# Hybrid attention, SSD and delta-net layer on one core: other PSUM banks for the first half's transposes, other buffers and a later request time around the second half's output projection

## The chip, the core and the metric

The kernel runs on one core of a Trainium2 chip. The metric is the device time of one execution in microseconds (us). TensorE (PE) does the matrix products, VectorE (DVE) and ScalarE (ACT) the elementwise work, GpSimd (POOL) some small operations; SyncE (SP) starts most transfers, and ACT starts the stores. Each engine takes its instructions in one fixed order, and each works through its own list without looking at what another engine's list holds, except where it waits for a semaphore.

## The reference

One layer on x of shape (1, 1024, 1024) in float32:

```
h    = rmsnorm(x);  p = h @ w_in
a    = sliding-window attention (4 heads, sinks, ALiBi)      256 columns
s    = Mamba-2 SSD                                           512 columns
g    = gated DeltaNet                                        256 columns
x1   = x + rmsnorm(concat[a, s, g] @ w_out)
h    = rmsnorm(x1)
out  = x1 + rmsnorm((silu(h @ w_gate) * (h @ w_up)) @ w_down)    FF = 2816
```

## The kernel before, in words

The 1024 rows are worked in two halves of 512 rows, each of 4 tiles of 128 rows (t = 0 to 3). Every matrix product is three passes over a float32r high part and low part ("hi" and "lo"): hi by hi, hi by lo, lo by hi. The split costs an ACT copy (hi) and a DVE subtraction (lo) for every operand block.

Phase 1 (`half`) makes the three mixers of a half and stores their outputs to DRAM as `mixd`. In the second half's order of work (`ORD[1]`) the steps end with `a0 a1 O a2 a3`: attention of tiles 0 and 1, then `O`, which is `block_first`, then attention of tiles 2 and 3. One attention tile (`att_tile`, twice a tile, once per key head) is: scores `as` on PE, mask and maximum on DVE (`asc`, `am`), exponentials on ACT, transposes `tp_p` on PE, a copy `apT` on ACT, the product `ao` on PE, the scaling `aout` on DVE, and a store of `aout` to `mixd`.

`block_first` is the first half's output projection: it multiplies the mixer output by `w_out` in four column groups g of 256 columns (`mm_o`, 24 matmuls for one g and one tile), and in g = 3, tile by tile, forms the first residual row `res`, its norm, a normalised row `o`, and after t = 1 and t = 3 the transposes `tp_f` of two tiles, whose evictions give `hhi_m` (ACT) and `hlo_m` (DVE). The early FFN products of the first half follow: `e00p` to `e11p` (`ffn_early`, pairs 0 and 1, 96 matmuls of 512 columns).

PSUM has eight banks. In phase 1 they are four pools of two: "mm" (projections, `mm_o`), "gd", "sd" (DeltaNet and SSD; "sd" also `ao`) and "at" (`as`, `tp_p`). A pool hands its two buffers out in the order in which the program is written, so an `as` of tile 2, written after `block_first`, gets a buffer that a `tp_f` written before it has held.

Phase 2 begins with the second half's output projection: the mixer output is read back (`mixn`, L1026 to L1030), transposed (`tp_m`, by `split_T`) into `mhi` and `mlo`, and multiplied by `w_out` (again `mm_o`, g = 0 to 3). Between the groups stand the early FFN products of pairs 2 to 5 (`e20p` to `e51p`, 192 matmuls). Then the rows are transposed (`tp_f`, L1096), combined into the operands of a Strassen form (`hx`, `T1` to `T4`), and 11 FFN pairs follow (`fg0p`, `fu0p` and on), whose raw weights `fg0r`, `fu0r` (512 KB loads) go into the four "nat" buffers of `npool`. In the kernel before, `mixn` lies in "nat" too, the second residual in "tmp", and all `w_out` pieces and all early weights pass through the three "wr" buffers of `wpool`.

What sets the order: the Tile framework's scheduler lists the instructions of every engine from the program, with priorities (`tc.high_priority`), buffer counts and a timeline model; the lists are fixed when the kernel is built.

## Time and profile before

| | us |
|---|---|
| median of 3 runs | 1301.12 (1297.75 to 1302.74) |
| the profiled execution | 1301.61 |
| its span, first to last instruction | 1299.8 |
| PE busy in the span | 1234.9 (95%) |
| DVE busy | 948.9 (73%) |
| ACT busy | 578.1 (44%) |
| mean granted PE clock | 0.970 of full speed |

The page cuts the span in 40 slices; PE is busy for 9 tenths or more in nearly all, and shows 6, 9 and 7 tenths in the three slices from 520 to 617 us, the crossing from the first half to the second, and 8 in the one from 682 to 715 us, the end of the second half's projection. Shares of busy time are averages over stages with different limits, so the stages are read apart from each other.

### The profile page before, as it was taken

The page shows a single profiled execution, that of the slowest core. Times are in us where ns is not written, and L with a number is a line of the kernel's source. Part 1 is how long each engine was busy: PE and PEld are TensorE (multiplying, and loading weights), DVE is VectorE, ACT ScalarE, POOL GpSimd, SP SyncE. Part 2 cuts the span into 40 slices and gives each one's busy share as a digit, 9 for nine tenths or more (in the row PEclk, how much of TensorE's full clock was granted, in tenths as well). Part 3 has the DMA queues.
Part 4 walks back from the last instruction along what each step waited for, and adds up shares of the span by engine and source line. Part 5 has one row for each costly group of instructions (what it writes and reads, how often), then busy time and mean ns, then how long its engine had stood idle before and what let it go on. Part 6 is the DMA issues. An engine that isn't in the chain of part 4 may idle for free.

```text
span 1299.8 us, 19149 instructions
## 1 busy us (share of the span) xinstructions
PE 1234.9 (95%) x6624; PEld 1028.3 (79%) x6624; DVE 948.9 (73%) x1898; ACT 578.1 (44%) x1269; POOL 225.3 (17%) x313
## 2 busy tenths in 40 slices
PE   5999999999998999697998999999999999999997
PEld 4878788887777889676996888888888887888885
DVE  5687996687799475644456999887777757767885
ACT  6454444445544343533436543433333343454561
POOL 3243554224355432200000000000000000000001
PEclk9899989999999999777998999999999999999999
DMA  7223332133323222535534356543333268676315
GB/s 234 74 70 85 86 89 65 48 103 89 96 77 80 76 91 74 174 96 196 170 106 139 121 189 224 187 138 114 100 111 99 72 217 311 190 218 230 98 57 194
DMA packets 161412, 168.57 MB, mean 130 GB/s; under 512 B 29566, under 2 KB 116890, under 8 KB 161316
## 3 DMA queue, kind: packets, MB, share of 16 engines
q1 hardware_dynamic: 143892, 133.53, 34.4%
q10 hardware_dynamic: 17424, 33.82, 7.0%
q8 instruction: 52, 0.85, 0.3%
q14 instruction: 44, 0.36, 0.1%
HBM read 127.21 MB, written 40.11 MB: 129 GB/s over the span
## 4 chain that ended last, share of the span: by engine, by line
PE 84%; DVE 7%; DMA 4%; ACT 2%; issue 1%; POOL 1%; ACTq 0%; SPq 0%; POOLq 0%; DVEq 0%
PE mm_p L1177 5%; PE mm_p L1179 5%; PE mm_p L1178 5%; PE mm_o L206 2%; PE mm_o L207 2%; PE mm_o L208 2%; PE gram L487 1%; DMA x<-in_x_dram 1%; PE mm_z L206 1%; DVE Tpr L513 1%; PE y L676 1%; DMA yb<-in_ffn_w_down_dram 1%; PE ao L755 1%; PE mm_z L207 1%; PE mm_z L208 1%
## 5 line engine op out<-in xcount | busy, mean ns | idle before, releaser
L169 POOL TENSOR_TENSOR rsq<-ssv,mhalf 128x1 f32<-128x1 f32 x32 | 19.8, 623 | 774.6 <-DVE ssv L259 774.5
L513 DVE TENSOR_TENSOR Tpr<-Tst,Wst 128x32 f32<-128x32 f32 (+30 forms) x62 | 49.0, 790 | 4.8 <-POOL Wst L508 4.1
L206 PE MATMUL mm_z<-wh_z,hhi_a 128*128 128x256 f32 x128 | 38.0, 297 | 0.0
L206 PE MATMUL mm_o<-wh_wo,hhi_m 128*128 128x256 f32 x128 | 36.5, 286 | 1.2 <-ACT junko L866 1.1
L207 PE MATMUL mm_o<-wl_wo,mhi 128*128 128x256 f32 x128 | 37.2, 292 | 0.2 <-DVE wl_wo L186 0.2
L208 PE MATMUL mm_o<-wh_wo,mlo 128*128 128x256 f32 x128 | 36.9, 290 | 0.0
L206 PE MATMUL mm_o<-wh_wo,mhi 128*128 128x256 f32 x128 | 36.8, 291 | 0.0
L208 PE MATMUL mm_z<-wh_z,hlo_a 128*128 128x256 f32 x128 | 36.6, 286 | 0.0
L207 PE MATMUL mm_z<-wl_z,hhi_a 128*128 128x256 f32 x128 | 36.6, 286 | 0.0
L208 PE MATMUL mm_o<-wh_wo,hlo_m 128*128 128x256 f32 x128 | 36.0, 281 | 0.0
L207 PE MATMUL mm_o<-wl_wo,hhi_m 128*128 128x256 f32 x128 | 35.9, 281 | 0.0
L185 ACT ACTIVATE wh_wo<-wr_wo 128x512 fp32r<-128x512 f32 x32 | 19.8, 629 | 34.0 <-DMA wr_wo<-in_w_out_dram 9.6
L186 DVE TENSOR_TENSOR wl_wo<-wr_wo,wh_wo 128x512 fp32r<-128x512 f32 x24 | 17.6, 743 | 16.8 <-ACT wh_wo L185 16.7
L515 DVE TENSOR_REDUCE Tst<-Tpr 128x16 f32<-128x32 f32 (+30 forms) x62 | 26.9, 433 | 0.6
L676 PE MATMUL y<-xs,sE 128*128 128x64 f32 x128 | 19.5, 283 | 7.6 <-DVE sE L669 7.6
L207 PEld LDWEIGHTS mm_o<-wl_wo,mhi 128*128 128x128 f32 x128 | 25.4, 198 | 0.8 <-DVE wl_wo L186 0.5
L206 PEld LDWEIGHTS mm_o<-wh_wo,mhi 128*128 128x128 f32 x128 | 25.2, 198 | 0.7 <-DVE mlo L236 0.3
L213 PE MATMUL mm_x<-hlo_a,wh_x 128*128 128x512 f32 x64 | 25.7, 402 | 0.0
L212 PE MATMUL mm_x<-hhi_a,wh_x 128*128 128x512 f32 x64 | 25.5, 399 | 0.0
L676 PEld LDWEIGHTS y<-xs,sE 128*128 128x128 f32 x128 | 18.2, 202 | 9.2 <-DVE sE L669 8.0
L206 PEld LDWEIGHTS mm_o<-wh_wo,hhi_m 128*128 128x128 f32 x128 | 24.1, 188 | 1.8 <-ACT junko L866 1.3
L214 PE MATMUL mm_x<-hhi_a,wl_x 128*128 128x512 f32 x64 | 25.5, 398 | 0.0
(1619 smaller groups left out, 4456.6 us busy)
## 6 DMA issues: line engine op xcount, KB each, us to landing
wr_wo<-in_w_out_dram SPq DMA_DIRECT2D x32, 256.0 KB
x<-in_x_dram SPq DMA_DIRECT2D x8, 512.0 KB
wr_x<-in_w_in_dram SPq DMA_DIRECT2D x16, 256.0 KB
wr_z<-in_w_in_dram SPq DMA_DIRECT2D x16, 256.0 KB
mixn<-mixd SPq DMA_DIRECT2D x16, 256.0 KB
resf<-x1d SPq DMA_DIRECT2D x8, 512.0 KB
wr_e<-in_ffn_w_gate_dram SPq DMA_DIRECT2D x12, 256.0 KB
wr_e<-in_ffn_w_up_dram SPq DMA_DIRECT2D x12, 256.0 KB
```

The costliest lines, as they stand in the source:

```text
L206: pe.matmul(ps, hi[:, tsl], whi, start=k == 0, stop=False)
L207: pe.matmul(ps, hi[:, tsl], wlo, start=False, stop=False)
L208: pe.matmul(ps, lo[:, tsl], whi, start=False, stop=k == len(wp) - 1)
L212: pe.matmul(ps, whi, hi, start=k == 0, stop=False)
L213: pe.matmul(ps, whi, lo, start=False, stop=False)
L214: pe.matmul(ps, wlo, hi, start=False, stop=k == len(wp) - 1)
L513: vec.tensor_tensor(pr[:, :, 0:i + 1], T[:, :, 0:i + 1], W[:, None, 0:i + 1, i].to_broadcast([P, CW, i + 1]), op=ALU.mult)
L515: vec.tensor_reduce(T[:, :, i], pr[:, :, 0:i + 1], axis=AX, op=ALU.add)
L676: pe.matmul(yd[:, j], E[:, j, :], xs[:, j], start=True, stop=True)
L1177: pe.matmul(ps[j], ah[:, s], bh, start=i == 0, stop=False)
L1178: pe.matmul(ps[j], ah[:, s], bl, start=False, stop=False)
L1179: pe.matmul(ps[j], al[:, s], bh, start=False, stop=i == NP - 1)
```

## The change

Five edits, all around the crossing from the first half to the second:

1. `block_first`'s transposes `tp_f` take buffers of "gd" and "mm" in place of "sd" and "at".
2. The second half's mixer output lies in eight "tmp" half-tiles. It is read by three transfers a tile in place of two (columns 512 to 1023, 256 to 511, and for all tiles last 0 to 255, the attention's columns), and transposed by one `split_T` over all four tiles (8 blocks of 128 x 512, the attention's blocks 0 and 1 last) in place of two over two tiles each (16 evictions of 128 x 256).
3. The second residual lies in "nat", one 512 KB load a tile in place of two of 256 KB.
4. The `w_out` pieces of g = 1 and g = 3 are split into "big" buffers in place of the six "wh" and "wl".
5. The raw early weights of pairs 2 to 5 go through "tmp" in place of "wr" and lose their high priority, and those of pairs 4 and 5 are written in the program after the projection, not in its g = 1.

```diff
--- before.py
+++ after.py
@@ -1,5 +1,5 @@
 import math
-from contextlib import ExitStack
+from contextlib import ExitStack, nullcontext
 
 import numpy as np
 import concourse.bass as bass
@@ -218,11 +218,11 @@
                  hp.tile([P, HT], F32R, tag="hlo", name=f"hlo_{name}{k}", bufs=KB))
                 for k in range(KB)]
 
-    def split_T(name, nats, t0, out, wcols, streams=("mm",)):
+    def split_T(name, nats, t0, out, wcols, streams=("mm",), ks=range(KB)):
 
         n = len(nats)
         s = slice(t0 * P, (t0 + n) * P)
-        for i, k0 in enumerate(range(0, KB, NT // n)):
+        for i, k0 in enumerate(ks[::NT // n]):
             p = mx(f"tp_{name}{t0}{k0}", streams[i % len(streams)])
             for e in range(NT // n):
                 for j in range(n):
@@ -879,7 +879,7 @@
                     else:
                         vec.tensor_scalar(o[t][e], src, r, None, op0=ALU.mult)
                 if t % 2:
-                    split_T(f"f{h}", [halves_of(o[t - 1]), halves_of(o[t])], t - 1, mT, 8, ("sd", "at"))
+                    split_T(f"f{h}", [halves_of(o[t - 1]), halves_of(o[t])], t - 1, mT, 8, ("gd", "mm"))
         return mT
 
 
@@ -905,12 +905,12 @@
             pe.matmul(ps, wlo[:, s], hi, start=False, stop=k == n - 1)
         return ps
 
-    def early_weights(w, i, e, tiles):
+    def early_weights(w, i, e, raw, tiles):
         n = f"e{i}{e}"
         parts = []
-        with tc.high_priority():
+        with tc.high_priority() if tiles is None else nullcontext():
             for h in range(2):
-                q = wpool.tile([P, WC], F32, tag="wr", name=f"wr_{n}{h}")[:, 0:HT]
+                q = raw(f"wr_{n}{h}")
                 q = q.rearrange("p (k c) -> p k c", k=4)
                 dma(q, w[h * HT:(h + 1) * HT, i * 256:i * 256 + P].rearrange("(k p) c -> p k c", p=P))
                 parts.append(split(f"{n}w{h}", q, tiles and tiles(f"{n}{h}")))
@@ -931,7 +931,7 @@
     mT_h0 = o0[0]
     for i in range(EARLY[0]):
         for e, w in enumerate((wg, wu)):
-            ffn_early(w, i, e, early_weights(w, i, e, None), lambda nm: mpool.tile(
+            ffn_early(w, i, e, early_weights(w, i, e, lambda nm: wpool.tile([P, WC], F32, tag="wr", name=nm)[:, 0:HT], None), lambda nm: mpool.tile(
                 [P, 4, P], F32, tag="Wn", name=nm, bufs=GT).rearrange("p a b -> p (a b)"), ("gd", "sd"))
     ph1.close()
 
@@ -950,6 +950,9 @@
 
     def big(nm, dt=F32R):
         return ph2.tile([P, HT], dt, tag="big", name=nm, bufs=BIG)
+
+    def big_pair(nm):
+        return big(f"{nm}h"), big(f"{nm}l")
 
     def tmp(nm):
         return ph2t.tile([P, HT], F32, tag="tmp", name=nm, bufs=TMP)
@@ -1022,18 +1025,26 @@
         return t
 
 
-    nats = []
+    nats, heads = [], []
     for t in range(NT):
-        mt = nat(f"mixn1{t}")
-        for e in range(2):
-            dma(mt[:, e * HT:(e + 1) * HT], mixd[NT + t][:, e * HT:(e + 1) * HT])
-        nats.append(cols_of(mt))
+        mt = [tmp(f"mixn1{t}{e}") for e in range(2)]
+        dma(mt[1], mixd[NT + t][:, HT:D])
+        dma(mt[0][:, 256:HT], mixd[NT + t][:, 256:HT])
+        nats.append(halves_of(mt))
+        heads.append(mt[0])
+    for t in range(NT):
+        dma(heads[t][:, 0:256], mixd[NT + t][:, 0:256])
     mT = [(big(f"mhi{k}"), big(f"mlo{k}")) for k in range(KB)]
-    for t0 in (0, 2):
-        split_T("m1", nats[t0:t0 + 2], t0, mT, 16, ("tp", "mm"))
+    split_T("m1", nats, 0, mT, 16, ("tp", "mm"), [2, 3, 4, 5, 6, 7, 0, 1])
     pm = pm_rows
     later = range(EARLY[0], sum(EARLY))
     early_w = {}
+
+    def weights_second(pairs):
+        for i in pairs:
+            for e, w in enumerate((wg, wu)):
+                early_w[i, e] = early_weights(w, i, e, tmp, big_pair)
+
     xts = []
     GW = 256
     ng = D // GW
@@ -1041,16 +1052,14 @@
     ss = [small.tile([P, ng], F32, tag=f"oss{ng}", name=f"oss1{t}", bufs=NT) for t in range(NT)]
     for g in range(ng):
         c0 = g * GW
-        wp = piece(f"wo1{g}", [(0, a["w_out"][0][:, c0:c0 + GW])], KB, GW)
+        wp = piece(f"wo1{g}", [(0, a["w_out"][0][:, c0:c0 + GW])], KB, GW, big_pair if g % 2 else None)
         if g == 0:
             for t in range(NT):
-                xts.append([tmp(f"res1{t}{e}") for e in range(2)])
-                for e in range(2):
-                    dma(xts[t][e], x_in[(NT + t) * P:(NT + t + 1) * P, e * HT:(e + 1) * HT])
+                xt = nat(f"res1{t}")
+                dma(xt, x_in[(NT + t) * P:(NT + t + 1) * P])
+                xts.append(pair_of(xt))
         if g == 1:
-            for i in later:
-                for e, w in enumerate((wg, wu)):
-                    early_w[i, e] = early_weights(w, i, e, lambda nm: (big(f"{nm}h"), big(f"{nm}l")))
+            weights_second(later[:-2])
         for t in range(NT):
             xt = xts[t]
             ps = ps_mm.tile([P, HT], F32, tag="mm", name=f"mm_o1{g}{t}")[:, 0:GW]
@@ -1086,6 +1095,7 @@
             for e, w in enumerate((wg, wu)):
                 ffn_early(w, i, e, early_w[i, e], tmp, ("f", "f"))
 
+    weights_second(later[-2:])
     early_second(later[:-2])
     f1 = []
     for k in range(KH):
```

The scheduler's lists move with it. On PE, attention of tiles 2 and 3 is the first place. In the kernel before its matmuls stand behind all of `block_first`, among the early FFN products (`e10p`); a last one of them and what follows:

```order
L904 MATMUL e10p_6643<-hlo_m_5608,wh_e10w_6631 128x512
L905 MATMUL e10p_6643<-hhi_m_5607,wl_e10w_6632 128x512
L755 MATMUL ao_6431<-av_5459,apT_6424 128x64 x4
L744 MATMUL tp_p_6459<-cst,asc_6439 128x128
L719 MATMUL as_6474<-ak_5413,aq_5333 128x256
L719 MATMUL as_6474<-ak_5413,aq_5374 128x256
L744 MATMUL tp_p_6459<-cst,asc_6439 128x128 x3
L755 MATMUL ao_6465<-av_5459,apT_6458 128x64 x4
L744 MATMUL tp_p_6493<-cst,asc_6473 128x128
L719 MATMUL as_6508<-ak_5413,aq_5333 128x256
```

With the change they stand ahead of it, between the last column group's products:

```order
L744 MATMUL tp_p_6459<-cst,asc_6439 128x128 x4
L719 MATMUL as_6474<-ak_5413,aq_5333 128x256
L719 MATMUL as_6474<-ak_5413,aq_5374 128x256
L755 MATMUL ao_6465<-av_5459,apT_6458 128x64 x4
L230 MATMUL tp_f_6233<-cst,o_5742 128x128
L230 MATMUL tp_f_6242<-cst,o_5742 128x128
L230 MATMUL tp_f_6251<-cst,o_6018 128x128
L230 MATMUL tp_f_6260<-cst,o_6018 128x128
L744 MATMUL tp_p_6493<-cst,asc_6473 128x128
L719 MATMUL as_6508<-ak_5413,aq_5333 128x256
L719 MATMUL as_6508<-ak_5413,aq_5374 128x256
L744 MATMUL tp_p_6493<-cst,asc_6473 128x128 x3
```

So the scores, transposes and products of attention move from behind the first half's transposes to before and between them.

The second place is PE at the third tile's product of the last column group (`mm_o_6271`). In the kernel before both remaining products run ahead of all transposes; the end of the second one and the first transposes:

```order
L207 MATMUL mm_o_6321<-wl_wo_6128,hhi_m_5615 128x256
L208 MATMUL mm_o_6321<-wh_wo_6127,hlo_m_5616 128x256
L230 MATMUL tp_f_6233<-cst,o_5742 128x128
L230 MATMUL tp_f_6242<-cst,o_5742 128x128
L230 MATMUL tp_f_6251<-cst,o_6018 128x128
L230 MATMUL tp_f_6260<-cst,o_6018 128x128
```

With the change the third tile's product stands behind the transposes of tiles 0 and 1, one of whose buffers it takes:

```order
L230 MATMUL tp_f_6242<-cst,o_5771 128x128
L744 MATMUL tp_p_6527<-cst,asc_6507 128x128 x3
L206 MATMUL mm_o_6271<-wh_wo_6109,hhi_m_5601 128x256
L207 MATMUL mm_o_6271<-wl_wo_6110,hhi_m_5601 128x256
L208 MATMUL mm_o_6271<-wh_wo_6109,hlo_m_5602 128x256
L206 MATMUL mm_o_6271<-wh_wo_6109,hhi_m_5603 128x256
```

The product of the third tile has moved from before the transposes of the first two tiles to after them.

The third place is DVE. In the kernel before the first operation on the raw FFN weights (`fg0t`) stands ahead of the evictions of the second half's mixer transposes (`mlo`):

```order
L186 TENSOR_TENSOR wl_wo_7082<-wr_wo_7083,wh_wo_7081 128x512
L994 TENSOR_TENSOR fg0t_8095<-fg0r_8089 128x512
L236 SCALAR_TENSOR_TENSOR mlo_6828<-tp_m_6843,ncol,mhi_6827 128x256
L995 TENSOR_TENSOR fg0r_8089<-fg0r_8089,fg0r_8090 128x4x128
L236 SCALAR_TENSOR_TENSOR mlo_6830<-tp_m_6843,ncol,mhi_6829 128x256
```

With the change it stands ahead of the norm and the normalised rows (`o`) of the second half's projection:

```order
L895 TENSOR_TENSOR e401l<-wr_e_7609,e401h 128x512
L997 TENSOR_TENSOR fg0t_8079<-fg0r_8073 128x512
L258 TENSOR_REDUCE ssv<-ss 128x1
L258 TENSOR_REDUCE ssv<-oss_6909 128x1
L259 TENSOR_SCALAR ssv<-ssv 128x1 x2
L895 TENSOR_TENSOR e410l<-wr_e_7615,e410h 128x512
L1084 TENSOR_SCALAR o_7321<-res_6937,rsq 128x512
L895 TENSOR_TENSOR e411l<-wr_e_7621,e411h 128x512
L1070 TENSOR_TENSOR o_7379<-mm_o_7554,pm_row_5686 128x256
```

The operation that needs the weight load has left the start of the second half's projection and stands now at its end.

## Rows read from the trace of the kernel before

**Rows 1.** Windows by stage: us, busy time (count) of five engines, PE clock, DMA share, GB/s.

```profile
500.00:535.30 35.30, 34.19 (x295) 33.98 (x294) 21.56 (x53) 13.50 (x38) 10.65 (x12) 1.00 0.28 87
535.30:553.40 18.10, 9.28 (x42) 6.80 (x40) 12.60 (x33) 12.00 (x33) 2.72 (x5) 0.61 0.65 209
553.40:579.00 25.60, 23.13 (x101) 17.58 (x102) 13.29 (x44) 10.85 (x32) 0.00 (x0) 0.83 0.26 80
579.00:595.00 16.00, 16.00 (x61) 12.80 (x61) 4.86 (x8) 3.99 (x7) 0.00 (x0) 0.85 0.82 276
595.00:609.20 14.20, 5.33 (x25) 3.65 (x23) 9.19 (x19) 6.39 (x15) 0.00 (x0) 0.70 0.42 140
609.20:686.70 77.50, 77.25 (x511) 71.72 (x511) 36.94 (x72) 31.75 (x78) 2.18 (x4) 0.97 0.43 136
686.70:704.80 18.10, 11.82 (x54) 8.94 (x52) 9.99 (x22) 11.90 (x24) 2.49 (x4) 0.81 0.39 130
704.80:765.00 60.20, 60.20 (x261) 49.07 (x262) 58.19 (x98) 31.62 (x56) 0.00 (x0) 1.00 0.51 164
```

**Rows 2.** Windows of 2 us, the same columns.

```profile
540.00:542.00 2.00, 1.22 (x6) 0.82 (x4) 1.36 (x3) 1.85 (x5) 0.00 (x0) 0.50 1.11 318
556.00:558.00 2.00, 2.00 (x8) 1.24 (x8) 0.51 (x2) 0.00 (x0) 0.00 (x0) 0.90 0.00 0
```

**Rows 3.** The chain that ended last: start us, us, what.

```profile
593.80 0.23 PE e11p L903
...
596.44 5.42 DMA fg0r<-in_ffn_w_gate_dram
...
609.79 0.21 PE mm_o L207
...
647.09 2.96 DMA wr_wo<-in_w_out_dram
```

**Rows 4.** Timeline of PE: start, us, instruction, count, idle before and its releaser.

```profile
532.37 0.39 PE L206 MATMUL mm_o<-wh_wo,hhi_m 128*128 128x256 f32 x1 [1.11 <-ACT junko L866]
...
535.18 0.28 PE L208 MATMUL mm_o<-wh_wo,hlo_m 128*128 128x256 f32 x1
...
550.57 2.82 PE L230 MATMUL tp_f<-cst,o 128*128 128x128 f32 x12 [3.57 <-DVE o L880]
...
561.82 1.13 PE L719 MATMUL as<-ak,aq 64*128 64x256 f32 x4
562.88 0.55 PE L744 MATMUL tp_p<-cst,asc 128*128 128x128 f32 x3
...
566.04 1.00 PE L755 MATMUL ao<-av,apT 128*128 128x64 f32 x8
...
603.17 1.09 PE L230 MATMUL tp_m<-cst,mixn 128*128 128x128 f32 x4 [7.11 <-issue]
```

**Rows 5.** Timeline of DVE, 518 to 612 us, the same columns.

```profile
525.72 0.42 DVE L864 TENSOR_TENSOR o<-mm_o,pm_row 128x256 f32<-128x256 f32 x1 [0.77 <-PE mm_o L208]
...
532.85 0.49 DVE L880 TENSOR_SCALAR o<-res,rsq 128x512 f32<-128x512 f32 x1
...
538.30 0.49 DVE L880 TENSOR_SCALAR o<-res,rsq 128x512 f32<-128x512 f32 x1 [0.66 <-POOL rsq L169]
...
544.28 0.48 DVE L880 TENSOR_SCALAR o<-res,rsq 128x512 f32<-128x512 f32 x1
...
550.02 0.48 DVE L880 TENSOR_SCALAR o<-res,rsq 128x512 f32<-128x512 f32 x1 [0.72 <-POOL rsq L169]
...
600.45 0.69 DVE L994 TENSOR_TENSOR fg0t<-fg0r 128x512 f32<-128x512 f32 x1 [3.89 <-DMA fg0r<-in_ffn_w_gate_dram]
```

**Rows 6.** Instructions on tile tp_m: duration ns (minimum, median, maximum), first and last start.

```profile
L236 DVE SCALAR_TENSOR_TENSOR hlo_m<-tp_m,ncol,hhi_m x8: 734/738/745, 452.7 to 467.5; 128x512 fp32r<-128x512 f32 x8
```

**Rows 7.** Timeline of PE, 686 to 706 us.

```profile
686.55 0.28 PE L208 MATMUL mm_o<-wh_wo,mlo 128*128 128x256 f32 x1
...
696.43 0.71 PE L1096 MATMUL tp_f<-cst,o 128*128 128x128 f32 x2 [3.64 <-DVE o L1075]
...
704.76 0.51 PE L903 MATMUL e50p<-hhi_m,e500h 128*128 128x512 f32 x1 [1.27 <-ACT e40s L922]
```

## The prediction

> **What bounds the kernel now.** I began with the busy time by stage [rows 1]. From 704.8 us on PE is busy all the time and DVE nearly so (58.19 of 60.20 us): there the PE products bound the kernel, and no edit touches them. The loss sits between 535.3 and 704.8 us. The stage 535.3 to 553.4 us has PE busy for 9.28 of 18.10 us, the stage 595.0 to 609.2 us for 5.33 of 14.20 us, the stage 686.7 to 704.8 us for 11.82 of 18.10 us. The stage 553.4 to 579.0 us looks busy, but at a clock of 0.83: it holds the four late attention tiles, whose parts wait for each other.
>
> The clock is the second loss [rows 2]. In the gaps it falls to half (0.50 at 540 us), and it is back only in 556 to 558 us (0.90), after PE has worked without a gap since 550.57 us. A 256-column product then takes 0.21 us [rows 3] in place of 0.117 us (24 from 532.37 to 535.18 us, first and last in [rows 4]).
>
> Then I read what ends each gap. The transposes of the first half wait for the normalised rows `o`, 3.57 us before the last [rows 4]. These four rows come 5.7 us apart (532.85, 538.30, 544.28, 550.02 us) [rows 5], since norm, residual and norm of one tile follow those of the tile before. The 7.11 us before `tp_m` [rows 4] is a DVE matter: `fg0t` waited 3.89 us for its load [rows 5], the evictions `mlo` stood behind it, and the load took 5.42 us [rows 3].
>
> **The change part by part.** The sum is made against the profiled execution, 1301.61 us; the median shown, 1301.12 us, is 0.5 us lower, and I don't correct for it. I place three moments: the end of the first half's transposes (553.4 us now), the first product of the second half's projection (609.2 us), and `e50p` (704.8 us), after which both kernels do the same.
>
> *First moment: other banks (edit 1).* Attention of tiles 2 and 3 no longer waits for `tp_f`, so it runs inside the last two column groups. The third tile's product in the last group now needs a buffer that a `tp_f` of tiles 0 and 1 holds, so the two pairs of transposes stand in line where they overlapped. Now: tile 3's product starts at 532.37 us after 1.11 us idle [rows 4], so tile 2's ended at 531.2 us, and with 2.8 us for 24 matmuls tile 1's ended at 528.4 us. Ahead of that end come two `as` (1.06 us each, start to start in [rows 4]), one `tp_p` (0.55) and one `ao` (1.00): 532.1 us. From there to the row `o` of tile 1 it takes 10.4 us now (528.4 to 538.8 us [rows 5]); attention's work on DVE and ACT stands in the same lists, which I put at 1.0 us (bounds: 0, and 4 us, two spacings less the 7.1 us below): 543.5 us. Twelve transposes take 2.8 us [rows 4], the last evictions 2.5 us more: an estimate, half of eight at the 0.74 us of [rows 6], which are twice as wide. So the third tile's product starts at 548.8 us. At half clock, after such gaps, its 24 matmuls take 5.1 us (0.21 each): 553.9 us. From a product's `o` to its normalised row the first tile took 7.1 us (525.72 to 532.85 us), with 0.5 us for the row itself: 561.5 us; the fourth comes 5.7 us later: 567.2 us. Transposes, 2.8 us, and a start of 0.5 us: **570.5 us, 17.1 us later than now**.
>
> *Second moment (edits 2 and 3).* From 553.4 to 609.2 us, 55.8 us pass now. Of these, 96 products of 512 columns stay, 22.4 us at 0.23 us [rows 3], with 1.7 us for a start at half clock (the clock is low for 4 us, so half of that, less the 0.3 us that 0.90 gives back). Attention (stage 553.4 to 579.0 us) is gone. Eight of the mixer's transposes go in between, 1.1 us for four at half clock [rows 4], so 1.1 us at full. The other 24 are paced by eight evictions of 512 columns at 0.74 us, 5.9 us [rows 6], and a first ACT copy of 0.7 us; the eight wide ones replace sixteen narrow ones. `fg0t` no longer stands ahead. The `mixn` loads must land by 583 us: they can start at 570 us, when the residual ahead of them in SP's list has a free "nat" buffer, and 12 issues and 2 MB at the 276 GB/s of 579 to 595 us [rows 1] take 8 us: they are hidden behind the first 48 products (11.2 us); if not, 1 to 5 us. Sum 31.8 us: **602.3 us, 6.9 us earlier than now**.
>
> *Third moment (edits 3, 4 and 5).* 95.6 us pass now. The products are the same 384, 192 less the 48 of `e50p` and `e51p`, and 32 transposes. Two things differ.
>
> First, the split of g = 1's weights stands in DVE's list behind the four rows `o` of g = 0, though "big" buffers are free: 0.4 us for the last row and 0.7 us for a split, so PE waits 1.1 us. The fourth piece needs a "wr" buffer that the first frees, and SP asks for it behind eight early loads that wait for `tp_m`; its load takes 2.96 us [rows 3] and both split halves 1.3 us, and PE runs out of covered products for about 1.6 us. That is 2.7 us for 0.2 us now; bounds 0 (all early) and 6 us (loads held up by the eight).
>
> Second, "nat" is held by the residual, so `fg0r` and `fu0r` can be asked for only as each tile's residual is done, and their first operations stand in DVE's list ahead of the later rows `o`. By DVE's pace of 0.6 us an operation (98 in 58.19 us [rows 1]) the 17 operations on weights between `fg0t` and the last `o` are 10.2 us, the four residual updates and small ones 4.8 us; four waits for loads of 5.42 us, of which all but 6.2 us in all lies beside the operations ahead. The last `o` so comes 21.9 us after the last product in place of 9.6 us (686.83 to 696.43 us [rows 7]). But PE has more to do meanwhile: 69 early products, 16.1 us, in place of 19, 4.4 us. Loss: 12.3 - 11.7 = 0.6 us; bounds -3 (no wait in the last loads) and 9 us (each of the last three waits its whole 5.42 us, of which half is covered).
>
> So **98.7 us in place of 95.6: 3.1 us lost**. The clock is taken alike: half speed for 5 us after 609 us, and again around 700 us. Edit 4 frees the six "wh" and "wl" for g = 0 and 2 and costs nothing itself: four pieces are split by the same operations. POOL and the ACT queue's stores keep their places.
>
> Sum: -6.9 + 3.1 = -3.8, and 1301.61 - 3.8 = **1297.8 us**, 0.3% less.
>
> **The rivals.** *The whole gain stays.* The second pair of rows overlaps attention as it did, which brings the first moment 4 us forward (the 1.0 us, and 3 us of the low clock), and the tail's waits are covered (3.1 us). Then 1301.61 - 3.8 - 7.1 = 1290.7 us. For it: all 25.6 us of the attention stage is no longer alone on the path. Against it: rows 5.7 us apart in every tile. This is what the Trainium skill, page "Perfetto Trace Analysis", section "Optimization Strategy", would lead to: find the gaps of the contended engine, make what ends them start sooner, and interleave stages with different limits. By that rule the gap before `tp_m`, 7.1 us, and the thin stage would go and nothing would come back. The trace shows the gaps; that what is moved brings gaps of its own no run here shows yet.
>
> *Two chains in line.* If attention's work on DVE and ACT and the weights' splits stretch each pair of rows to the length that both pairs have now, 18.1 us (535.3 to 553.4 us [rows 1]), then from 532.1 us: 550.2; two products at half clock with an `ao` between, 12.2: 562.4; 18.1: 580.5 us, 10.0 us later than forecast: 1307.8 us. It decides from the point where the first half's transposes end after 574.3 us (no gain), and is slower than 0.5% from 580.8 us. For it: DVE's list has attention between the residual's steps. Against it: those 18.1 us serve four tiles, and here a pair is two.
>
> *The stall has only moved.* `fg0t`'s wait goes from `mlo` to the last rows, with nothing to cover it: the tail costs the 6.9 us that were gained, 1301.6 us. For it: the same 5.42 us load ahead of a chain that PE waits for. Against it: 69 products of cover.
>
> **How the numbers follow.** A measurement of this kernel tells some 0.5%, 6.5 us, from no change. Forecast 0.46 (1293 to 1303 us); whole gain 0.31; two chains 0.13; moved stall 0.10. Faster by over 0.5% (under 1294.6 us) takes the second case and a ninth of the first: 0.36. Slower by over 0.5% (over 1307.6 us) is half of the third and unknown costs beside: 0.12. The same: 0.52. The range reaches from 1287 us (the whole gain with the lower bounds) to 1307 us, just short of the two chains.
>
> **What would show it.** Right: `as` of tiles 2 and 3 ahead of 545 us; a PE gap of 2 to 4 us before the third tile's last product; the first half's transposes done near 570 us; no gap of 7 us before `tp_m`, and the second projection's first product near 602 us; DVE waiting for `fg0r` near the end of that projection; `e50p` near 701 us. Wrong: `mixn` landing after 583 us, an early second moment with a late `e50p`, or any difference after `fg0p` (DVE has 2 us to spare in 60).

## The result, and the profile after

The changed kernel takes 1282.29 us (median of 4 runs, 1280.08 to 1286.78), the kernel before beside it 1300.34 us (1297.75 to 1302.74): ratio 0.9866, 95% interval 0.9832 to 0.9900, so 18 us or 1.3% less. The forecast was 1297.8 us with a range from 1287 us: the change is a clear gain and the forecast called it too small to measure.

The profiled execution is the fastest of the four (span 1278.3 us, 1299.8 before). 2.6 us of the 21.5 us between the two spans are not the change's: before 500 us nothing was edited, yet the same product `S` starts at 502.30 us before and at 499.68 us after. PE works through the same list of products up to there, and its clock came up earlier in this execution (granted 0.50 before and 0.93 after in 30 to 40 us). So the three moments are compared from that `S`, by adding 2.62 us:

| moment | before | forecast | after | after + 2.62 | against the forecast |
|---|---|---|---|---|---|
| first early product (`e00p`) | 553.4 | 570.5 | 562.14 | 564.8 | -5.7 |
| second projection's first product | 609.2 | 602.3 | 592.39 | 595.0 | -7.3 |
| `e50p` | 704.8 | 701.0 | 681.35 | 684.0 | -17.0 |

The windows that answer to [rows 1], of the kernel after, in the same columns:

```profile
500.00:529.70 29.70, 29.70 (x246) 28.62 (x245) 20.25 (x56) 11.65 (x35) 8.74 (x10) 1.00 0.27 81
529.70:545.20 15.50, 11.53 (x54) 8.99 (x52) 11.15 (x37) 10.62 (x32) 1.65 (x3) 0.67 0.45 149
545.20:562.10 16.90, 9.85 (x72) 9.41 (x73) 10.09 (x26) 9.78 (x25) 2.18 (x4) 0.85 0.50 159
562.10:592.40 30.30, 27.70 (x131) 22.02 (x129) 13.52 (x24) 12.68 (x24) 0.00 (x0) 0.97 0.89 289
592.40:664.00 71.60, 70.50 (x490) 65.43 (x491) 34.69 (x70) 30.45 (x79) 3.14 (x5) 1.00 0.39 123
664.00:681.35 17.35, 14.39 (x72) 10.71 (x70) 13.81 (x29) 11.30 (x21) 2.69 (x3) 1.00 0.58 188
681.35:741.50 60.15, 60.15 (x260) 49.00 (x261) 57.48 (x97) 31.39 (x56) 0.00 (x0) 1.00 0.49 163
```

The loss now sits between 529.7 and 562.1 us, where PE is busy for 21.4 of 32.4 us: the two pairs of rows in line, as forecast. Behind it the thin stages are gone, and the clock column reads 0.97 to 1.00 where [rows 1] has 0.70 to 0.97. From `S` to `e50p` PE works through the same matmuls (1059 records in each trace) in 202.5 us before and 181.7 us after. Of the 20.8 us between them, 10.7 are busy time that the same matmuls no longer take (174.65 to 163.99 us, at a mean clock of 0.88 and 0.95), and 10.1 are idle time (27.8 to 17.7 us).

The timeline of PE after, the rows that answer to [rows 4] and [rows 7]:

```profile
545.20 0.36 PE L206 MATMUL mm_o<-wh_wo,hhi_m 128*128 128x256 f32 x1 [1.08 <-DVE hlo_m L236]
...
555.70 0.65 PE L230 MATMUL tp_f<-cst,o 128*128 128x128 f32 x4 [3.74 <-ACT o L878]
...
559.66 2.82 PE L230 MATMUL tp_f<-cst,o 128*128 128x128 f32 x12 [3.31 <-DVE o L880]
...
589.00 2.63 PE L230 MATMUL tp_m<-cst,mixn 128*128 128x128 f32 x16 [1.85 <-DVE mlo L236]
592.39 0.36 PE L206 MATMUL mm_o<-wh_wo,mhi 128*128 128x256 f32 x1 [0.75 <-ACT mhi L235]
...
605.73 0.39 PE L206 MATMUL mm_o<-wo110h,mhi 128*128 128x256 f32 x1 [0.97 <-ACT junko L1072]
...
674.76 0.44 PE L1106 MATMUL tp_f<-cst,o 128*128 128x128 f32 x2 [0.52 <-DVE o L1084]
...
681.35 0.50 PE L903 MATMUL e50p<-hhi_m,e500h 128*128 128x512 f32 x1 [1.27 <-ACT e40s L922]
```

The third tile's product waits 1.08 us for the evictions of the first transposes, the wait that edit 1 adds (2 to 4 us in the forecast's signs). The 7.11 us ahead of `tp_m` are 1.85 us now, and the 3.64 us ahead of the last rows' transposes 0.52 us.

The clock, in short windows: first two of the kernel before (ahead of its second projection's start PE was busy for 5.33 of 14.20 us [rows 1]) and two at its end, then the kernel after.

```profile
609.00:611.00 2.00, 2.00 (x10) 1.79 (x9) 1.25 (x4) 1.22 (x3) 0.00 (x0) 0.50 0.27 32
611.00:613.00 2.00, 2.00 (x11) 2.00 (x10) 0.36 (x1) 0.00 (x0) 0.00 (x0) 0.50 1.06 367
...
692.00:696.00 4.00, 0.56 (x2) 0.28 (x2) 2.02 (x6) 1.97 (x6) 0.76 (x2) 1.00 1.00 368
696.00:700.00 4.00, 2.79 (x11) 2.12 (x12) 1.28 (x3) 2.64 (x5) 0.00 (x0) 0.54 0.09 36
```

```profile
540.00:542.00 2.00, 2.00 (x12) 2.00 (x12) 1.06 (x4) 1.63 (x6) 0.12 (x1) 0.50 0.00 0
542.00:544.00 2.00, 2.00 (x13) 1.88 (x12) 1.12 (x4) 1.59 (x5) 0.00 (x0) 0.67 0.83 223
544.00:546.00 2.00, 0.92 (x9) 0.84 (x8) 1.72 (x5) 2.00 (x6) 0.00 (x0) 1.00 0.21 72
...
590.00:594.00 4.00, 3.11 (x19) 2.02 (x18) 3.56 (x6) 2.36 (x4) 0.00 (x0) 1.00 0.69 199
...
674.00:678.00 4.00, 2.50 (x17) 1.46 (x15) 3.81 (x7) 3.53 (x6) 0.00 (x0) 1.00 0.86 263
```

Before, the two thin stretches were each followed by the lower level (0.50 and 0.54; 0.50 is 1.2 GHz). After, PE came through gaps of 1.85 and 0.75 us, and through a tail with 2.5 busy us in 4, at the full level (1.00, 2.4 GHz). And at 544 us, after 4 us of unbroken attention and transposes, the level was back before the third tile's product began.

### The profile page after: what moved, and what is told of

Read it like the earlier page. It is cut to its first block, busy times and chain, and to the rows that moved or that the text cites. A ratio compares the mean times of both kernels' runs of the same rounds, so it can differ in the third digit from the quotient of the medians.

```text
span 1278.3 us, 19099 instructions
## 1 busy us (share of the span) xinstructions
PE 1223.0 (96%) x6624; PEld 1017.1 (80%) x6624; DVE 946.3 (74%) x1890; ACT 574.6 (45%) x1261; POOL 224.4 (18%) x313
## 4 chain that ended last, share of the span: by engine, by line
PE 82%; DVE 9%; DMA 4%; ACT 2%; issue 1%; POOL 1%; SPq 0%; ACTq 0%; POOLq 0%; DVEq 0%
PE mm_p L1187 5%; PE mm_p L1188 5%; PE mm_p L1189 5%; PE mm_o L206 2%; PE mm_o L208 2%; PE mm_o L207 2%; DVE Tpr L513 1%; PE gram L487 1%; DMA yb<-in_ffn_w_down_dram 1%; PE y L676 1%; PE ao L755 1%; PE as L719 1%; PE mm_z L206 1%; PE mm_z L207 1%; PE mm_z L208 1%
## 5 line engine op out<-in xcount | busy, mean ns | idle before, releaser
L207 PE MATMUL mm_z<-wl_z,hhi_a 128*128 128x256 f32 x128 | 36.5, 285 | 0.0
L1070 DVE TENSOR_TENSOR o<-mm_o,pm_row 128x256 f32<-128x256 f32 x16 | 6.8, 424 | 27.9 <-PE mm_o L208 27.9
L185 ACT ACTIVATE wh_wo<-wr_wo 128x512 fp32r<-128x512 f32 x24 | 15.1, 630 | 24.7 <-DMA es<-e00s 5.0
L206 PEld LDWEIGHTS mm_z<-wh_z,hhi_a 128*128 128x128 f32 x128 | 24.8, 194 | 0.5
L207 PEld LDWEIGHTS mm_z<-wl_z,hhi_a 128*128 128x128 f32 x128 | 24.6, 192 | 0.3
L208 PEld LDWEIGHTS mm_z<-wh_z,hlo_a 128*128 128x128 f32 x128 | 24.7, 193 | 0.0
L208 PEld LDWEIGHTS mm_o<-wh_wo,hlo_m 128*128 128x128 f32 x128 | 24.1, 188 | 0.3 <-issue 0.3
L207 PEld LDWEIGHTS mm_o<-wl_wo,hhi_m 128*128 128x128 f32 x128 | 24.1, 188 | 0.0
```

The lines of the kernel that those rows point to most:

```text
L206: pe.matmul(ps, hi[:, tsl], whi, start=k == 0, stop=False)
L207: pe.matmul(ps, hi[:, tsl], wlo, start=False, stop=False)
L208: pe.matmul(ps, lo[:, tsl], whi, start=False, stop=k == len(wp) - 1)
```

## The experiments

Fifteen kernels were timed beside these two. From each profile I read three stretches: **front**, from the `S` named above to `e00p`; **middle**, from there to the second projection's first product; **end**, from there to `e50p`. Ratios are against the kernel before, run beside each. A stretch is read from one execution: eight kernels have the same PE list from `S` to `e00p` (all with edit 1 as changed), and their fronts reach from 62.5 to 65.0 us. In the edits, `...` and `<...>` stand for code that is left out.

| kernel | median us | ratio (95%) | front | middle | end |
|---|---|---|---|---|---|
| before | 1300.3 | | 51.1 | 55.8 | 95.6 |
| changed, edits 1 to 5 | 1282.3 | 0.9866 (0.9832 to 0.9900) | 62.5 | 30.3 | 89.0 |
| edit 1 alone | 1294.8 | 0.9961 (0.9946 to 0.9976) | 65.0 | 37.6 | 94.2 |
| edit 3 alone | 1301.2 | 1.0014 (0.9997 to 1.0031) | 51.3 | 49.0 | 101.1 |
| edits 4, 5 alone | 1300.0 | 1.0013 (1.0003 to 1.0024) | 51.1 | 60.1 | 91.6 |
| changed, 1 undone | 1289.3 | 0.9911 (0.9886 to 0.9935) | 51.9 | 50.1 | 90.7 |
| changed, 2 undone | 1287.1 | 0.9916 (0.9894 to 0.9938) | 64.4 | 32.5 | 89.3 |
| changed, 3 undone | 1287.2 | 0.9899 (0.9876 to 0.9921) | 64.4 | 29.7 | 91.2 |
| changed, 4 and 5 undone | 1295.3 | 0.9964 (0.9951 to 0.9977) | 64.7 | 29.7 | 101.3 |
| changed, 4 undone | 1280.2 | 0.9862 (0.9832 to 0.9893) | 63.7 | 31.1 | 85.0 |
| changed, 5: all pairs asked early | 1306.3 | 1.0047 (1.0030 to 1.0065) | 63.4 | 30.3 | 109.9 |
| changed, 5: raw in `wr` again | 1288.5 | 0.9928 (0.9903 to 0.9952) | 63.4 | 30.3 | 96.2 |
| gd banks alone | 1277.2 | 0.9833 (0.9814 to 0.9851) | 59.1 | 29.9 | 88.9 |
| gd banks, four `wr` | 1284.4 | 0.9888 (0.9867 to 0.9910) | 58.5 | 30.7 | 88.4 |
| gd banks, QK raw | 1275.6 | 0.9810 (0.9795 to 0.9826) | 58.8 | 30.4 | 89.1 |
| gd banks, 4 undone | 1270.3 | 0.9773 (0.9758 to 0.9788) | 58.8 | 29.5 | 85.7 |
| gd banks, QK raw, 4 undone | 1274.1 | 0.9800 (0.9784 to 0.9816) | 59.7 | 29.7 | 85.4 |

By their ratios the parts alone give about -5 us, +2 and +2 us, the whole -17: the edits need each other. Edit 3 alone costs 2 us and its undoing 5, edits 4 and 5 alone cost 2 us and their undoing 13 (edit 2 alone was not run).

**Edit 1 alone, on the kernel before.**

```diff
-split_T(..., t - 1, mT, 8, ("sd", "at"))
+split_T(..., t - 1, mT, 8, ("gd", "mm"))
```

> The kernel before with edit 1 alone (first half's transposes in the banks gd and mm). Theory A (the order around attention is the main gain: attention of the last two tiles leaves the early products' stretch, where it ran at a clock of 0.83): the first early product starts near 565 us in place of 553.4, the stretch from there to the second projection shrinks from 55.8 to 36 to 42 us (the wait for the load of fg0t ahead of the evictions mlo may stay, with the half clock after it), the time is 8 to 13 us under the kernel before: 1287 to 1292 us. Theory B (the gain lies in the other buffers and weights, edits 2 to 5): what is won behind is lost in front; within 3 us of the kernel before: 1297 to 1303 us.

Measured: 1294.8 us. The middle shrinks by 18.2 us as theory A has it, but the front grows by 13.9, so the balance lies between the theories. The 7.1 us gap ahead of `tp_m` stays, and DVE shows the same cause as in [rows 5]:

```profile
594.21 0.69 DVE L994 TENSOR_TENSOR fg0t<-fg0r 128x512 f32<-128x512 f32 x1 [3.91 <-DMA fg0r<-in_ffn_w_gate_dram]
594.82 0.48 DVE L236 SCALAR_TENSOR_TENSOR mlo<-tp_m,ncol,mhi 128x256 fp32r<-128x256 f32 x1
```

**Edit 1 undone** in the changed kernel.

```diff
-split_T(..., t - 1, mT, 8, ("gd", "mm"))
+split_T(..., t - 1, mT, 8, ("sd", "at"))
```

> The changed kernel with edit 1 undone (banks sd and at again), edits 2 to 5 kept. Theory A: 8 to 13 us slower than the changed kernel, 1290 to 1295 us, with attention of the last two tiles between the early products again; what stays of the gain, 5 to 10 us, is the 7.1 us gap ahead of the second half's transposes. Theory B: 0 to 3 us slower than the changed kernel, 1282 to 1285 us.

Measured: 1289.3 us, just below theory A's interval. The front is short again (51.9 us), the middle takes 50.1 us with attention in it. Edit 1 is worth 4 to 7 us either way.

**Edits 4 and 5 undone.**

```diff
-wp = piece(..., KB, GW, big_pair if g % 2 else None)
+wp = piece(..., KB, GW)
-with tc.high_priority() if tiles is None else nullcontext():
+with tc.high_priority():
-early_w[i, e] = early_weights(w, i, e, tmp, big_pair)
+early_w[i, e] = early_weights(w, i, e, <wr tile>, big_pair)
-weights_second(later[:-2])
+weights_second(later)
...
-weights_second(later[-2:])
```

> The changed kernel with edits 4 and 5 undone (odd w_out pieces in wh and wl, early weights of pairs 2 to 5 through wr, with high priority, all asked for at the second column group). The stretch from the second projection's first product to e50p took 95.6 us before and 89.0 us in the changed kernel. Theory C (this stretch became shorter because PE comes into it without a gap and at full clock, and the early products cover the rows' waits; the weights' buffers count for little): 88 to 91 us, time 1281 to 1285 us. Theory D (it became shorter because the weights come in another order through other buffers): back to 94 to 97 us, time 1287 to 1290 us.

Measured: 1295.3 us, and the end takes 101.3 us, longer than in either theory and longer than before. PE's timeline behind the last product:

```profile
674.62 0.28 PE L208 MATMUL mm_o<-wh_wo,mlo 128*128 128x256 f32 x1
683.87 0.69 PE L1105 MATMUL tp_f<-cst,o 128*128 128x128 f32 x2 [4.14 <-DVE o L1084]
692.52 0.69 PE L1105 MATMUL tp_f<-cst,o 128*128 128x128 f32 x2 [7.97 <-ACT o L1083]
```

The last row comes 17.6 us after the last product (674.90 to 692.52 us), 19 early products (4.4 us) cover some of it, and PE waits 12.1 us. Edit 3 without edits 4 and 5 is a loss at this place.

**Edit 3 undone.**

```diff
-xt = nat(f"res1{t}")
-dma(xt, x_in[(NT + t) * P:(NT + t + 1) * P])
-xts.append(pair_of(xt))
+xts.append([tmp(f"res1{t}{e}") for e in range(2)])
+for e in range(2):
+    dma(xts[t][e], x_in[(NT + t) * P:(NT + t + 1) * P, e * HT:(e + 1) * HT])
```

> The changed kernel with edit 3 undone (the second half's residual in two tmp half tiles and two loads a tile; so the raw FFN weights fg0r and fu0r find free nat buffers before the second projection). Theory E (the wait of the evictions mlo for that load is what edit 3 took away): DVE waits for fg0r again ahead of the second half's transposes, a PE gap of 3 to 7 us and half clock behind it, 1285 to 1292 us. Theory C (the crossing has already moved the transposes behind the load, and with the weights ready early the last rows come sooner): no gap over 2 us, the tail's waits fall from 3.0 us of PE to 1 us or less, 1279 to 1283 us.

Measured: 1287.2 us. Theory E's time, but not its mechanism: the middle is 29.7 us and PE waits only 1.84 us ahead of the last `tp_m`. With the mixer's output in `tmp`, `nat` is free for `fg0r` long before. The rows are covered as theory C has it (no gap over 0.5 us behind the last product but the 1.26 us ahead of `e50p`), but four waits of 0.5 to 1.0 us come between the column groups, one of them for a piece of `w_out`.

**Edit 3 alone:** these lines the other way round, in the kernel before.

> The kernel before with edit 3 alone (second half's residual in nat). Theory L (edit 3 gives in one place and takes in the other): the evictions mlo no longer stand behind fg0t, so the gap of 7.1 us ahead of the second half's transposes shrinks to under 3 us, but the last rows come late with 19 early products to cover them, 10 to 13 us of PE gaps at the end in place of 4.2: from the first product to e50p 99 to 103 us in place of 95.6, time 1297 to 1302 us. Theory E (edit 3 is a gain of its own): 1291 to 1295 us.

Measured: 1301.2 us, theory L. The gap ahead of `tp_m` falls from 7.11 to 2.46 us, the end grows to 101.1 us with waits of 4.09 and 7.80 us for rows.

**Edits 4 and 5 alone,** in the kernel before.

> The kernel before with edits 4 and 5 alone, with its residual in tmp half tiles. The residual edit undone showed the last rows covered but the last w_out pieces late. Theory K (cover is worth what the rows' waits are, here 4.2 us of PE gaps at the end): the end's gaps go, some 3 us of waits for late w_out pieces come, and the gap of 7.1 us ahead of the second half's transposes stays: 0 to 5 us under the kernel before, 1294 to 1299 us. Theory D (the weights' buffers and loads are worth 12 us by themselves): 1286 to 1290 us.

Measured: 1300.0 us, 1 us above theory K's interval. The end wins 3.9 us as theory K has it, but the middle loses 4.3: the gap ahead of `tp_m` grows to 11.17 us, and DVE waits 8.20 us for `fg0r` (3.89 us in [rows 5]). Eight early loads now stand ahead of it in SP's list; it is asked for at 597.52 us (595.98 before), and DVE has it 6.7 us later (4.5 before).

```profile
604.26 0.69 DVE L997 TENSOR_TENSOR fg0t<-fg0r 128x512 f32<-128x512 f32 x1 [8.20 <-DMA fg0r<-in_ffn_w_gate_dram]
```

**Edit 5, the time of asking undone:** all pairs at the second column group.

```diff
-weights_second(later[:-2])
+weights_second(later)
...
-weights_second(later[-2:])
```

> The changed kernel with one part of edit 5 undone: the weights of pairs 4 and 5 are asked for at the second column group too, not after the projection. The list of PE then has all early products of pairs 2 to 4 ahead of the last projection product, where the changed kernel has 69 of them behind it. Theory K (what edits 4 and 5 bring is cover: early products kept for the time in which the last rows are normalised): PE waits 12 to 17 us for the rows behind the last product in place of 1.3 us, from the first product to e50p 98 to 104 us in place of 89.0, time 1291 to 1297 us. Theory D (they bring it by the weights' buffers and loads, which stay as they are here): 88 to 91 us, time 1281 to 1285 us.

Measured: 1306.3 us, 24 us more than the changed kernel by this edit alone. Nothing is left behind the last product, and PE stands for 17 us; its clock is 0.62 from there to `e50p`. This is theory K, larger than expected, with the low clock on top.

```profile
677.16 0.28 PE L208 MATMUL mm_o<-wo136h,mlo 128*128 128x256 f32 x1
677.28 0.38 PE L1105 MATMUL tp_f<-cst,o 128*128 128x128 f32 x2
681.27 0.44 PE L1105 MATMUL tp_f<-cst,o 128*128 128x128 f32 x2 [3.60 <-DVE ssv L259]
688.60 0.98 PE L1105 MATMUL tp_f<-cst,o 128*128 128x128 f32 x2 [6.89 <-ACT o L1083]
696.04 0.69 PE L1105 MATMUL tp_f<-cst,o 128*128 128x128 f32 x2 [6.46 <-DVE o L1084]
```

**Edit 4 undone:** `w_out` pieces in `wh` and `wl` only.

```diff
-wp = piece(..., KB, GW, big_pair if g % 2 else None)
+wp = piece(..., KB, GW)
```

> The changed kernel with edit 4 alone undone: all w_out pieces in the wh and wl buffers. PE's list then has even more early products behind the last projection product (some 115 in place of 69), but the last two column groups' pieces follow each other through the same buffers. Theory K (cover decides): waits for the rows at the end under 2 us, a few us of waits for late pieces between the column groups, time 1282 to 1287 us. Theory D (the weights' buffers are what edits 4 and 5 bring): 1289 to 1295 us.

Measured: 1280.2 us, below both theories. With 113 early products behind the last product, the end takes 85.0 us and has one wait over 0.4 us. Cover decides, as theory K has it, but the late pieces that it expected do not show: no wait comes between the column groups. Edit 4 brings nothing in time (the intervals overlap the changed kernel's), and in the end stretch it costs 4 us (89.0 against 85.0; 88.9 against 85.7 with the gd banks alone).

```profile
651.43 0.28 PE L208 MATMUL mm_o<-wh_wo,mlo 128*128 128x256 f32 x1
680.59 1.24 PE L1106 MATMUL tp_f<-cst,o 128*128 128x128 f32 x8 [0.32 <-ACT h L1109]
683.09 0.64 PE L903 MATMUL e50p<-hhi_m,e500h 128*128 128x512 f32 x1 [1.27 <-ACT e40s L922]
```

**Edit 5, the raw buffers undone:** raw weights of pairs 2 to 5 through `wr`.

> The changed kernel with the raw early weights of pairs 2 to 5 in the three wr buffers again, in place of tmp; when they are asked for stays as changed. Theory K: cover stays (some 60 early products behind the last projection product), waits for the rows at the end under 4 us; w_out pieces and early weights share three buffers, which costs 0 to 4 us: 1282 to 1286 us. Theory D: 1288 to 1295 us.

Measured: 1288.5 us, at theory D's lower end. Cover is there (some 60 products), but DVE waits for `fg0r` between the rows, and the last row comes 19.3 us after the last product (664.57 to 683.84 us): PE waits 4.55 us, and its mean clock in this stretch is 0.96 in place of 1.00. In the changed kernel SP has asked for all early loads by 595.2 us; here the last eight stand at 646 to 668 us, among those of `fg0r`. So the raw buffers are worth some 6 us too, through the times at which the loads are asked for.

```profile
674.00 0.69 DVE L998 TENSOR_TENSOR fg0r<-fg0r,fg0r 128x512 f32<-128x512 f32 x1 [3.66 <-DMA fg0r<-in_ffn_w_gate_dram]
```

**Edit 2 undone:** `mixn` in `nat`, two calls of `split_T` with two tiles each.

```diff
-mt = [tmp(f"mixn1{t}{e}") for e in range(2)]
+mt = nat(f"mixn1{t}")
...
-split_T("m1", nats, 0, mT, 16, ("tp", "mm"), [2, 3, 4, 5, 6, 7, 0, 1])
+for t0 in (0, 2):
+    split_T("m1", nats[t0:t0 + 2], t0, mT, 16, ("tp", "mm"))
```

> The changed kernel with edit 2 undone: the second half's mixer output in the four nat tiles again, two loads a tile, and two calls of split_T on two tiles each, with 16 evictions of 256 columns; the residual, still in nat, must follow it. PE's list is that of the changed kernel up to the order of these transposes. Theory P (with the residual in nat nothing stands ahead of the evictions any more, so edit 2 is worth only the narrower evictions): from the first early product to the second projection 31 to 34 us in place of 30.2, time 1283 to 1286 us. Theory Q (the mixer's output must wait for a nat buffer of the first half's residual and lands too late, or holds up the residual and the FFN weights behind it): 35 us or more there, or over 5 us of waits for the rows at the end, time 1287 to 1294 us.

Measured: 1287.1 us. By the stretches it is theory P (middle 32.5 us, end 89.3 us): the wider evictions are worth 2.3 us. The rest lies where PE works through the changed kernel's list: 1.9 us in the front (64.4 against 62.5 us), where ACT waits 2.98 us for a load of `e00w` in place of 1.45, and 2.0 us behind `e50p`.

**The gd banks alone,** in the changed kernel.

```diff
-split_T(..., t - 1, mT, 8, ("gd", "mm"))
+split_T(..., t - 1, mT, 8, ("gd",))
```

> The changed kernel with the first half's transposes in the two gd banks alone, so the third tile's last product needs no buffer that a transpose holds. In the instruction lists that product stands ahead of the first transposes, the attention of the last two tiles stays ahead of them too, and the two pairs of normalised rows overlap again. Theory G (the wait for that buffer put the pairs in line, which cost 8 to 11 us in front): from the last Z of the first half's scan to the first early product it takes 41 to 47 us in place of 52.2 (41.4 in the kernel before), time 1272 to 1279 us. Theory H (the chain of norms is bound by DVE and ACT, which do attention and the weights' splits besides): 49 to 53 us, time 1279 to 1285 us.

Measured: 1277.2 us. The time is theory G's; the first early product comes 48.8 us after the last `Z`, 3.4 us sooner than in the changed kernel but not as soon as hoped. Putting the pairs in line cost that much: PE's idle time from `S` to `e00p` falls from 11.0 to 7.3 us, and it was 9.9 us in the kernel before.

**Four `wr` buffers beside it** (the pool's `bufs=3` turned to 4).

> As the version with the two gd banks alone, and the raw weights' pool wr with four buffers in place of three. In that version and in the changed kernel ACT waits 1.5 to 3.1 us for the load of the second half of e00w, with the square of the first tile's product queued behind it, since that load needs a raw buffer which the split of the last w_out piece frees. Theory M (this load stands in the path of the first normalised row): from the last Z of the scan to the first transpose 22 to 25 us in place of 26.2, the first early product 2 to 4 us sooner, time 1273 to 1276 us. Theory N (the rows of the last tiles are bound by DVE and ACT later on, so an earlier first row is waited away): the first transpose comes sooner, but the first early product by less than 1 us: 1276.5 to 1279 us.

Measured: 1284.4 us. The larger pool moved the order in the whole first half, and `S` starts at 510.70 us, 8.4 us later than with three (499.6 to 505.1 us in all other kernels). The load's wait is gone and the front takes 58.5 us in place of 59.1, as theory N has it; with another order all through, this is no clean test of it.

**QK buffers for the raw weights of pairs 0 and 1.**

```diff
-early_weights(w, i, e, <wr tile>, None)
+early_weights(w, i, e, <tile of mpool, tag "QK", bufs=GT>, None)
```

> The two gd banks, and the raw early weights of pairs 0 and 1 in the four QK buffers, which the scan no longer needs then, in place of wr; nothing ahead of 495 us changes. Theory M (the load of e00w stands in the path of the first normalised row, since its raw buffer frees late): ACT no longer waits 2.5 us for it, the first early product comes 1.5 to 4 us sooner after the last Z of the scan (48.8 us there), time 1273 to 1275.7 us. Theory N (later rows are bound by DVE and ACT): less than 1 us, 1276 to 1279 us.

Measured: 1275.6 us, just inside theory M's interval, but the front is 58.8 us against 59.1: theory N. The load's wait is gone (ACT, first the gd banks alone, then with QK), but the first transposes come 37.5 us after `S` in place of 36.5: the order of attention's products changed too, and ACT now waits 2.06 us for `tp_p`.

```profile
529.91 0.63 ACT L894 ACTIVATE wh_e00w<-wr_e 128x512 fp32r<-128x512 f32 x1 [2.46 <-DMA wr_e<-in_ffn_w_gate_dram]
```

```profile
524.34 0.61 ACT L894 ACTIVATE wh_e00w<-wr_e 128x512 fp32r<-128x512 f32 x1
```

**The gd banks with edit 4 undone,** and **with QK buffers as well**.

> The two gd banks alone for the first half's transposes, and edit 4 undone. If the two add up (they lie in different stretches, and the second projection's stretch took 85.0 us in the run with edit 4 undone and 88.9 us with the gd banks): some 4 us less than the version with the gd banks, 1272 to 1275 us. If the gain of edit 4's undoing was chance (its median was 2 us under the changed kernel, within the spread), or is given back behind e50p: 1275.5 to 1278.5 us.

> Both together: gd banks, QK buffers for the raw weights of pairs 0 and 1, edit 4 undone. If all three parts add up: 1269 to 1273 us. If the front is bound by DVE and ACT: as the version without the QK buffers, 1272 to 1276 us.

Measured: 1270.3 us and 1274.1 us. The first is the fastest kernel of this study, 30 us or 2.3% under the kernel before. The two parts add up: 7 us by the medians where 4 were expected, of which the stretches show 3.7 (3.2 of them in the end). The QK buffers add nothing to it.

## Why the prediction was wrong

The direction of each step was right but for the last, and every size was too dear. `e50p` came 17.0 us sooner than forecast; 5.7 us of that arose up to the first moment, 1.6 up to the second and 9.7 up to the third.

**First moment, forecast 17.1 us later, measured 11.4.** The chain is the one forecast: attention ahead of 545 us, the third tile's product behind the first transposes, two pairs in line. Its start agrees (product forecast at 548.8 us, measured 545.20 + 2.62 = 547.8). Then "At half clock, after such gaps, its 24 matmuls take 5.1 us" failed: they took 3.1 us (545.20 to 548.30 us, DVE's `o`), since attention and transposes had kept PE going just before. "The fourth comes 5.7 us later" failed: 4.2 us.

```profile
548.30 0.42 DVE L864 TENSOR_TENSOR o<-mm_o,pm_row 128x256 f32<-128x256 f32 x1 [1.70 <-PE mm_o L208]
...
554.92 0.49 DVE L880 TENSOR_SCALAR o<-res,rsq 128x512 f32<-128x512 f32 x1 [0.63 <-POOL rsq L169]
...
559.12 0.49 DVE L880 TENSOR_SCALAR o<-res,rsq 128x512 f32<-128x512 f32 x1 [0.72 <-POOL rsq L169]
```

The 5.7 us came from a stretch in which DVE did splits of weights between the rows and the evictions `hlo_m` of the first pair's transposes; here one split stands between the two rows. Two sums of the forecast are also off as written: half of eight evictions at 0.74 us is 3.0 us and not 2.5, and in the third moment 10.2, 4.8 and 6.2 us add to 21.2 and not 21.9.

I also missed the load of `e00w` in this chain: ACT waits for it ahead of the first tile's square, 1.45 us here and up to 3.7 us in the experiments. It counts, as far as eight traces can show: in the eight kernels with the same PE list in front, the front grows with this wait (62.5 us at 1.45, 63.4 at 2.46, 64.4 at 2.98, 65.0 at 3.68). With the gd banks alone it does not (59.1 us at 2.46, 58.8 at 3.22 with edit 4 undone), so the QK run, made there, does not speak for the changed kernel.

**Second moment, middle forecast 31.8 us, measured 30.25.** Right: `fg0t` left the path, `mixn` was asked for from 562.6 us on, its first transposes ran at 574.1 us without a wait, and the clock was 0.97.

**Third moment, end forecast 98.7 us, measured 89.0.** This step failed most, in three terms.
- "The clock is taken alike": PE's busy time there is 84.9 us in place of 89.0, 4.1 us less for the same work, since neither dip came.
- The waits for rows. I put the last `o` 21.9 us after the last product; it came 17.1 us after (657.64 to 674.76 us). My 69 early products cover 16.1 us, so 1 us is left, and the profile shows 0.52 us. The cover was counted rightly; the chain was 4.8 us too long, because DVE waited for loads in it 1.8 us (the two lines below; 0.69 us more lay just ahead of the last product) and not 6.2.
- The two waits for g = 1, 2.7 us in the forecast, were one of 0.97 us.

```profile
672.09 0.69 DVE L997 TENSOR_TENSOR fu0t<-fu0r 128x512 f32<-128x512 f32 x1 [1.25 <-DMA fu0r<-in_ffn_w_up_dram]
...
673.62 0.69 DVE L998 TENSOR_TENSOR fu0r<-fu0r,fu0r 128x512 f32<-128x512 f32 x1 [0.58 <-DMA fu0r<-in_ffn_w_up_dram]
```

The experiments bear the cover out, at about the same chain:

| kernel | last product to last row, us | early products between | waits for rows, us |
|---|---|---|---|
| changed | 17.1 | 69 (16.1 us) | 0.5 |
| 4 and 5 undone | 17.6 | 19 (4.4 us) | 12.1 |
| edit 3 alone | 17.4 | 19 (4.4 us) | 11.9 |
| all pairs early | 18.6 | 0 | 17.0 |

So edit 3's price is real, and it is edit 5 that pays it, by the time at which it asks for the weights: with edits 4 and 5 undone this stretch is 12 us longer, with edit 4 alone undone 4 us shorter. Between two terms that nearly cancel, an error of 4.8 us in one turned the sign.

**The rivals.** "The whole gain stays" came nearest, at 1290.7 us, 8 us too high, in part because it too kept the clock's dips (4.1 us). Its covered tail came true and the overlap of the second pair of rows with attention did not, so that its number came nearest is partly luck. It was the case that the Trainium skill leads to, page "Perfetto Trace Analysis", section "Optimization Strategy": find what ends the gaps of the contended engine and make it start sooner. For the gap before `tp_m` the trace agrees (7.11 to 1.85 us). Taken alone the rule can mislead: with all weights asked for sooner, the work that filled a later gap was gone, and the kernel was 24 us slower. "Two chains in line" did not happen: the pairs stand in line, as in the forecast, but neither took the 18.1 us that this case adds. It was 15.5 us from the end of the second tile's product to the start of the third's (529.7 to 545.2 us), and 10.2 us from the end of the last product to `e00p` (552.0 to 562.1 us). "The stall has only moved" did not happen.

One sign that I named as wrong appears: 1.9 us were given back behind `e50p` (595.0 us to the end before, 596.9 after). It is not a wait: the list of PE is the same in both, and PE's busy time there rises by 2.1 us (584.64 to 586.76 us), spread over the whole stretch. It is not tied to an edit that I can name: other kernels have 595.1 us (gd banks alone) or 598.9 us (edit 2 undone). It stays open.

With the gd banks the front is still 8 us longer than before, but PE has more to do in it, since attention of tiles 2 and 3 has moved there: it is busy for 51.7 of 59.05 us, before for 41.2 of 51.1 us (changed kernel: 51.4 of 62.5 us). Open is why the load of `e00w`, asked for 23.6 us after `S` in all eight kernels, comes up to 2.2 us later in some.

## What to carry to other kernels

When a change lengthens a chain at the end of a stage, count two things: the chain from the last product to its last dependent, and the independent matmuls that the list leaves behind that product; the wait is the difference, and the order of requests for the next weights may decide it more than any buffer. Price TensorE's clock anew where a change closes or opens a thin stretch, since a gap costs again in the work behind it. And before giving a tile another PSUM bank, look who else needs that bank next: here two banks that no product was waiting for beat four.

## What the runs showed that I had not expected

- More banks were slower. The transposes in two `gd` banks took 1277.2 us, in `gd` and `mm` 1282.3 us. The Trainium skill, page "Perfetto Trace Analysis", section "Matmuls", says that independent groups should rotate through different PSUM banks; here two of the four belonged to the pool of the product that had to run next, and rotating through the other two alone won 5 us.
- The clock held through short gaps (1.85 us and 0.75 us at 589 to 592 us, 1.00) and fell after the nearly idle 4 us of the kernel before (0.56 us busy in 692 to 696 us, then 0.54).
- A larger pool for raw weights (four buffers in place of three) cost some 8 us in the first 500 us (`S` at 510.70 in place of 502.29 us): PE's order changed from its first products on, and one stretch (200 to 250 us) ran at a clock of 0.90 in place of 1.00.
